# The samples' attention steps through its caches two sequences at a time instead of one

## Chip, cores, metric

One core of a Trainium2 chip runs the whole program. The metric is the device time of one execution in microseconds; the kernel before takes 2231.66 us (median of 3 runs, 2231.16 to 2231.71).

## What is computed

One layer of a decoder with a pair of half-step SwiGLU FFNs around a mixing block, for a prompt of 1024 tokens and for 8 sample sequences of 4 new tokens each. The part that matters here is the mixing block's softmax attention (8 heads of 64, three dilated windows). The prompt attends within itself; each sample sequence attends to its own cached keys and values, of which 896 positions fall in some window:

```python
s = jnp.einsum('bthd,btjhd->bthj', q, kg) * (Dh ** -0.5)
s = jnp.where(valid[None, :, None, :], s, -jnp.inf)
m = jnp.max(s, axis=-1, keepdims=True)
p = jnp.exp(s - m)
den = jnp.sum(p, axis=-1)
o = jnp.einsum('bthj,btjhd->bthd', p, vg) / den[..., None]
```

The second head group (gated linear attention), the FFNs and the output steps are untouched.

## The kernel before

Python generators, called streams, issue the instructions of the mixing block; each `yield t, wait` hands TensorE's place in the program to another stream. `Merge.run` (L767) is a planner that runs while the program is built: it keeps a clock, adds `t` to it and to the stream's `used`, holds the stream back until `wait` has passed, and then takes, of the streams that are ready, the one with the least `used / share`. So the order on each engine is fixed when the program is built, and the engines run it strictly in that order.

Four streams matter. `project` makes the projections (L883: twelve matmuls per turn). `attend` (L1421) is the prompt's attention, eight heads of seven tiles; a step issues score matmuls `st` (L1505, L1506), matmuls `sm` for the maxima of a later head (L1453, none in the last twelve steps), and, one or two steps late, the weighted sums `nd` (L1532) of tiles that VectorE has masked (L1516, L1518) and ScalarE has exponentiated (L1519). It loads the next heads' operands with DMAs on SP's queue (L1438 to L1444, L1395, L1397). `attend_sample` (L1603) works on two groups of four sequences. `scores` multiplies the group's queries with the cached keys: for each of four quarters and each of four sequences it takes a key tile `kc` of 128x4x224 numbers (448 KB) and issues four matmuls that each fill 32 of the array's 128 columns (L1641). `sums` does the same with value tiles `vc` (also 448 KB), seven matmuls each (L1689). `turn` and `turn_back` are transposes between them, `finish` the division at the end. All these tiles come from one ring of four buffers (`KV = 4`): SP issues a tile's DMA once the matmuls on the tile four places earlier are done. `mix_ahead` (L1766) starts the output projection on heads that are ready (L1791, `acc_wo`), from step 46 of attention on, and `mix_out` continues it: it loads the residual `h` (L1802), adds the results to it (L1820) and also multiplies the samples' rows (L1841, `acc_wos`).

Both `scores` and `sums` yield once per sequence, 64 times in all:

```python
                    yield 0.8, 0.5
```

One such turn is called a visit below: 32-column matmuls of the samples between full-width matmuls of another stream. A group's second scores begin before its first sums: `attend_sample` takes eight turns of `scores(1)` before it transposes group 0's weights.

Of the kernel before, what the change touches and what calls it, by code (L numbers as in the profile page):

```python
# [1602 lines left out]
def attend_sample(k, a):  # L1603


    nc = k.nc
    qs, ks = k.qs, k.ks
    att = k.new[:, 512:640].rearrange("p (a t) -> p a t", a=4)
    st = [Head(), Head()]

    def prepare(g):
        S = st[g]
        qz = S.qz = k.sa.tile([P, 5, 4, 32], F32, name=f"qz{g}", tag="qz", bufs=2)
        nc.gpsimd.memset(qz, 0.0)
        for hh in range(2):
            r = slice(64 * hh, 64 * hh + 64)
            src = qs[r, :, g * 16:g * 16 + 16].rearrange("p a (b t) -> p a b t", t=TS)
            nc.vector.tensor_copy(qz[r, 4].rearrange("p a (b h t) -> p a b h t", h=2, t=TS)[:, :, :, hh], src)
            for b in range(4):
                c0 = b * 8 + hh * TS  # L1620
                nc.vector.tensor_copy(qz[r, b, :, c0:c0 + TS], src[:, :, b])

    def fetch():
        g, hf, qu, b = order.pop(0)
        kt = k.sa.tile([P, 4, 224], F32, name=f"kc{g}{hf}{qu}{b}", tag="kv", bufs=KV)
        nc.sync.dma_start(kt, a["c_k"][g * 4 + b, 2 * hf + qu])
        keys.append(kt)

    def scores(g):
        S = st[g]  # L1630
        qz = S.qz
        m = S.m = k.sa.tile([P, 4], F32, name=f"sm{g}", tag="smx", bufs=2)
        for hf, (c0, c1) in enumerate(((0, 448), (448, NPOS + NS))):
            sc = k.sy.tile([P, 512], F32, name=f"ss{g}{hf}", tag="y")
            for qu in range(2):
                for b in range(4):
                    if not keys:
                        fetch()
                    kt = keys.pop(0)
                    for pr in range(4):  # L1640
                        nc.tensor.matmul(sc[32 * pr:32 * pr + 32, qu * 224:qu * 224 + 224], qz[:, b, pr], kt[:, pr],  # L1641
                                         start=b == 0, stop=b == 3, skip_group_check=True)
                    yield 0.8, 0.5
            if hf:
                for pr in range(4):
                    nc.tensor.matmul(sc[32 * pr:32 * pr + 32, 448:448 + NS], qz[:, 4, pr], ks[:, pr], start=True,
                                     stop=True, skip_group_check=True)
            else:
                S.s = k.sa.tile([P, NPOS + NS], F32, name=f"s{g}", tag="ssb")
            nc.vector.tensor_tensor_reduce(S.s[:, c0:c1], sc[:, :c1 - c0], k.mC[:, c0:c1], 1.0, -3e38, ALU.add,  # L1650
                                           ALU.max, accum_out=m[:, hf:hf + 1])
            if g == 0:
                if hf:
                    nc.vector.tensor_copy(k.mC[:, NPOS:NPOS + NS], k.mC[:, NPOS + NS:])
                else:
                    prepare(1)
            yield 0.3, 1.2
        nc.vector.tensor_tensor(m[:, 2:3], m[:, 0:1], m[:, 1:2], op=ALU.max)
        nc.vector.tensor_scalar(m[:, 2:3], m[:, 2:3], -1.0, None, op0=ALU.mult)
        nc.scalar.activation(S.s, S.s, AF.Exp, bias=m[:, 2:3], accum_out=m[:, 3:4])  # L1660
        yield 0.0, 0.5

    def turn(g, c):
        S = st[g]
        if c == 0:
            S.pT = k.pT
        ps = k.sm.tile([P, 512], F32, name=f"spt{g}{c}", tag="m")
        for i in range(4):
            w = min(P, NPOS + NS - (c + i) * P)
            nc.tensor.transpose(ps[:w, i * P:(i + 1) * P], S.s[:, (c + i) * P:(c + i) * P + w], k.ident)  # L1670
        if c == 0:
            nc.scalar.activation(k.pT[:, 0:4], ps.rearrange("p (c q) -> p c q", q=P), AF.Copy)
        else:
            nc.scalar.activation(k.pT[:, 4:7], ps[:, :3 * P].rearrange("p (c q) -> p c q", q=P), AF.Copy)
            nc.scalar.activation(k.pT[:NS, 7], ps[:NS, 3 * P:], AF.Copy)
        yield 0.9, 0.5

    def sums(g, pieces):
        S = st[g]
        if 0 in pieces:  # L1680
            S.pv = k.sy.tile([P, 512], F32, name=f"spv{g}", tag="y")
        for piece in pieces:
            for b in range(4):
                vt = k.sa.tile([P, 7, P], F32, name=f"vc{g}{b}{piece}", tag="kv", bufs=KV)
                nc.sync.dma_start(vt, a["c_v"][g * 4 + b, piece])
                for i in range(7):
                    c, pr = divmod(7 * piece + i, 4)
                    q = slice(32 * pr, 32 * pr + 32)
                    nc.tensor.matmul(S.pv[q, b * P:(b + 1) * P], k.pT[:, c, q], vt[:, i], start=b == 0 and c == 0,  # L1689
                                     stop=False, skip_group_check=True)  # L1690
                yield 0.8, 0.5
        if 3 not in pieces:
            return
        for pr in range(4):
            q = slice(32 * pr, 32 * pr + 32)
            nc.tensor.matmul(S.pv[q].rearrange("p (b d) -> p b d", d=P), k.pT[:NS, 7, q],
                             k.vs[:, None, pr * P:(pr + 1) * P].broadcast_to([NS, 4, P]), start=False, stop=True,
                             skip_group_check=True)
        yield 0.9, 0.5

    def finish(g):
        S = st[g]
        mE = k.sa.tile([P, 512], F32, name=f"mE{g}", tag="kv", bufs=KV)
        nc.sync.dma_start(mE, a["c_mE"])
        e = k.sa.tile([P, 640], F32, name=f"se{g}", tag="qz", bufs=2)[:, :512]
        nc.vector.tensor_tensor(e, S.pv, mE, op=ALU.mult)
        o = k.new[:, 640:704]
        nc.vector.tensor_reduce(o, e.rearrange("p (g d) -> p d g", d=64), mybir.AxisListType.X, ALU.add)
        nc.vector.reciprocal(S.m[:, 3:4], S.m[:, 3:4])
        nc.vector.tensor_scalar(o, o, S.m[:, 3:4], None, op0=ALU.mult)  # L1710
        yield 0.0, 1.0

    def turn_back(g, ps):
        nc.tensor.transpose(ps[:64, :P], k.new[:, 640:704], k.ident)
        for hh in range(2):
            nc.scalar.activation(
                att[64 - 64 * hh:128 - 64 * hh, :, g * 16:g * 16 + 16].rearrange("p a (b t) -> p a b t", t=TS),
                ps[:64, :P].rearrange("p (a b h t) -> p a b h t", a=4, h=2, t=TS)[:, :, :, hh], AF.Copy)

    def sample_end():  # L1720
        turn_back(1, k.acc.tile([P, 512], F32, name="sot1", tag="acc"))
        nc.vector.tensor_tensor(k.xs[:, 4:], *(x[:, 4:, SEQ:].bitcast(F32) for x in (k.xh, k.xl)), op=ALU.add)

    k.sample_end = sample_end
    def part_0():
        while k.held:
            yield None
        turn_back(0, k.sx.tile([P, 512], F32, name="sot0", tag="x"))
        yield 0.2, 0.5

    early, late = (0, 1, 2), (3,)
    order = [(g, hf, qu, b) for g in range(2) for hf in range(2) for qu in range(2) for b in range(4)]
    keys = []
    for _ in range(KV):
        fetch()
    prepare(0)
    yield 0.0, 9.0
    yield from scores(0)
    second = scores(1)
    for _ in range(8):  # L1740
        yield next(second)
    yield from turn(0, 0)
    yield from turn(0, 4)
    yield from second
    yield from sums(0, early)
    yield from turn(1, 0)
    yield from sums(0, late)
    yield from finish(0)
    yield from turn(1, 4)
    yield from sums(1, early)  # L1750
    yield from part_0()
    yield from sums(1, late)
    yield from finish(1)
# [519 lines left out]
def build(tc, a):  # L2273
# [155 lines left out]
    with tc.manual_schedule(engines=ENGINES):  # L2429
# [39 lines left out]
        nc.sync.dma_start(k.mC, a["c_mC"])  # L2469
        k.pT = k.sa.tile([P, PC + 1, P], F32, name="pT")  # L2470
        samples = Stream(attend_sample(k, a), 140)
        issue.run(proj, att, samples, until=lambda: proj.done)
        less_w(0)
# [180 lines left out]
```

## Time and profile before

| | |
|---|---|
| runs | 2231.16, 2231.66, 2231.71 us |
| profiled execution | 2235.7 us, span 2233.5 us |
| TensorE busy | 2164.3 us (97%) |
| VectorE, ScalarE, GpSimd busy | 1479.8, 814.2, 614.7 us |
| TensorE's granted clock, mean | 0.986 |
| samples' attention | first visit at 1099.8 us, last at 1291.7 us |

Times in the rows are microseconds from the span's start. A matmul in float32 leaves two records, so a visit of four matmuls has 8 and one of seven has 14; the duration of a record includes the time that it overlaps its neighbours, so the cost of a piece is read from start to start. The profile names what an idle engine waited for; TensorE's idle time is the one that counts as long as the chain that ends last runs over it.

### The profile page before, as it was taken

To read this page: it belongs to the slowest core of one execution; us is meant where nothing else is said; L and a number is where in the kernel's file an instruction comes from. 1 tells how busy PE (TensorE), PEld (TensorE's weight loads), DVE (VectorE), ACT (ScalarE), POOL (GpSimd) and SP (SyncE) were. 2 spreads that over 40 slices of the span, in tenths; PEclk is the share of its full clock that TensorE was granted. 3 is DMA by queue.
4 is the path that set the end of the run, shared out by engine and by line. 5 is a ranking of instruction groups with operands and counts; after the bars stand their busy time and mean duration, and the time that the engine had idled before them with its cause. 6 is when DMAs were issued, how large, how long until landed. Compare 5 with 4: busy or idle time off the path is not lost.

```text
span 2233.5 us, 40152 instructions
## 1 busy us (share of the span) xinstructions
PE 2164.3 (97%) x16446; PEld 1769.2 (79%) x16446; DVE 1479.8 (66%) x2472; ACT 814.2 (36%) x1377; POOL 614.7 (28%) x446
## 2 busy tenths in 40 slices
PE   7999999999999999989999999999999999999996
PEld 5788888877777899979877877778888887777875
DVE  7855655658888845675267545966565567888866
ACT  4433333333121634432145523433343333112554
POOL 0456656640000001100124400265665651000000
PEclk9999999999999999989999999999999999999998
DMA  3377676639683311134988742177667648775112
GB/s 118 114 260 247 230 255 237 221 136 411 229 296 114 115 41 35 66 115 158 285 229 245 216 168 105 50 243 260 243 223 260 239 146 329 307 264 198 67 48 78
DMA packets 139848, 424.48 MB, mean 190 GB/s; under 512 B 18480, under 2 KB 39600, under 8 KB 129040
## 3 DMA queue, kind: packets, MB, share of 16 engines
q1 hardware_dynamic: 130400, 340.49, 43.3%
q0 software_dynamic: 4096, 76.81, 10.2%
q10 hardware_dynamic: 5168, 4.61, 0.6%
q8 instruction: 129, 2.11, 0.4%
q14 instruction: 55, 0.45, 0.1%
HBM read 312.15 MB, written 176.75 MB: 219 GB/s over the span
## 4 chain that ended last, share of the span: by engine, by line
PE 60%; DVE 7%; ACT 4%; DMA 4%; issue 3%; POOL 0%; SPq 0%; DVEq 0%; ACTq 0%; POOLq 0%
PE acc_a_f L174 10%; PE acc_c_f L174 10%; PE acc_b_f L174 8%; PE acc_d_f L174 6%; PE acc_m L883 5%; PE acc_wo L1791 3%; PE acc_e_f L174 3%; PE nd L1532 2%; PE acc_b L94 2%; PE st L1505 1%; DMA QA<-d_q 1%; PE sm_f L315 1%; PE acc_k L873 1%; PE sd_f L552 1%; PE st L1506 1%
## 5 line engine op out<-in xcount | busy, mean ns | idle before, releaser
L281 POOL TENSOR_TENSOR S_f<-raw_gu_f,S_f 128x512 f32<-128x512 f32 x40 | 59.5, 1487 | 320.7 <-DVE wl_f_a L296 320.7
L296 DVE TENSOR_TENSOR wl_f_a<-raw_gu_f,wh_f_a 128x1024 fp32r<-128x1024 f32 x44 | 55.9, 1273 | 113.0 <-ACT wh_f_a L295 113.0
L354 ACT ACTIVATE g_f<-acc_a_f 128x512 f32<-128x512 f32 x44 | 26.3, 597 | 241.5 <-PE acc_a_f L174 240.2
L883 PE MATMUL acc_m<-wh_m,xh_mx 128*128 128x256 f32 x384 | 112.6, 293 | 0.0
L276 POOL TENSOR_TENSOR S_f<-raw_gu_f 128x512 f32<-128x512 f32 x40 | 54.1, 1351 | 204.0 <-DMA raw_gu_f<-w_gu 203.8
L883 PE MATMUL acc_m<-wl_m,xh_mx 128*128 128x256 f32 x384 | 109.5, 285 | 0.0
L883 PE MATMUL acc_m<-wh_m,xl_mx 128*128 128x256 f32 x384 | 109.0, 284 | 0.0
L174 PE MATMUL acc_b_f<-xd_f,wh_f_s 128*128 128x512 f32 x320 | 101.2, 397 | 3.9 <-DVE c_f L338 3.9
L174 PE MATMUL acc_b_f<-xd_f,wh_f_a 128*128 128x512 f32 x320 | 104.1, 406 | 0.0
L2061 POOL TENSOR_TENSOR ho_f<-ho_f,rbc 128x256 f32<-128x256 f32 x2 | 1.7, 886 | 363.9 <-DVE rbc L189 363.9
L174 PE MATMUL acc_b_f<-xc_f,wh_f_s 128*128 128x512 f32 x320 | 99.5, 392 | 2.2 <-DVE U_f L338 2.2
L560 ACT ACTIVATE wo_f_wh<-wr_f 128x1024 fp32r<-128x1024 f32 x34 | 36.0, 1058 | 144.3 <-DVE wr_f L338 56.7
L357 ACT ACTIVATE g_f<-g_f 128x512 f32<-128x512 f32 x44 | 27.9, 633 | 148.6 <-DVE g_f L338 148.6
L679 DVE SCALAR_TENSOR_TENSOR ho_f<-acc_d_f,ho_f 128x512 f32<-128x512 f32 x88 | 60.3, 688 | 32.2 <-PE acc_d_f L174 27.7
L560 ACT ACTIVATE wo_f_wl<-wr_f 128x1024 fp32r<-128x1024 f32 x34 | 36.0, 1059 | 124.5 <-DVE wr_f L338 34.1
L296 DVE TENSOR_TENSOR wl_f_s<-S_f,wh_f_s 128x1024 fp32r<-128x1024 f32 x40 | 76.9, 1924 | 5.3 <-ACT wh_f_s L295 5.3
L361 POOL TENSOR_TENSOR t_f<-c_f,t_f 128x512 f32<-128x512 f32 x44 | 76.3, 1733 | 7.9 <-issue 4.0
L883 PEld LDWEIGHTS acc_m<-wh_m,xh_mx 128*128 128x128 f32 x384 | 73.5, 191 | 3.8 <-issue 1.8
L174 PEld LDWEIGHTS acc_b_f<-xd_f,wh_f_s 128*128 128x128 f32 x320 | 60.6, 190 | 19.4 <-issue 5.6
L174 PE MATMUL acc_a_f<-xh_f,wh_f_a 128*128 128x512 f32 x176 | 70.2, 399 | 5.9 <-ACT xh_f L242 5.9
L360 POOL TENSOR_TENSOR c_f<-g_f,c_f 128x512 f32<-128x512 f32 x40 | 72.0, 1799 | 11.1 <-DVE c_f L338 11.0
L883 PEld LDWEIGHTS acc_m<-wh_m,xl_mx 128*128 128x128 f32 x384 | 73.9, 192 | 0.0
(620 smaller groups left out, 6738.4 us busy)
## 6 DMA issues: line engine op xcount, KB each, us to landing
raw_gu_f<-w_gu SPq DMA_DIRECT2D x42, 1024.0 KB, 5.4
xo_f_xh<-d_hid SPq DMA_DIRECT2D x36, 1024.0 KB, 10.2
xo_f_xl<-d_hid SPq DMA_DIRECT2D x34, 1024.0 KB, 8.1
o_kw<-k_win POOLq DMA_DIRECT2D x8, 4088.0 KB, 15.7
o_vw<-v_win POOLq DMA_DIRECT2D x8, 4088.0 KB, 15.8
d_hid<-c_f SPq DMA_DIRECT2D x88, 256.0 KB, 3.8
d_hid<-hi_f_t SPq DMA_DIRECT2D x88, 256.0 KB, 2.3
wr_f<-w_d SPq DMA_DIRECT2D x40, 512.0 KB, 6.2
```

What stands on the lines that cost most here:

```text
L94: k.nc.tensor.matmul(ps[:, :n], w[:, kt, col:col + P], x[:, kt, cs], start=kt == 0 and i == 0, stop=kt == nk - 1 and i == 2)
L174: k.nc.tensor.matmul(ps, w, x, start=first and n + i == 0, stop=last and n == len(kts) - 1 and i == 2, skip_group_check=True)
L276: pool(q.S[:, 0], q.A[:, 2], q.A[:, 3], op=ALU.add)
L281: pool(q.S[:, 1], q.A[:, 1], q.S[:, 1], op=ALU.subtract)
L296: dve(wl[:, b], src, wh[:, b].bitcast(F32), op=ALU.subtract)
L360: h1 = lambda u: pool(unit(u).c21, unit(u).g1, unit(u).c21, op=ALU.mult)
L361: sub = lambda x, y, z: pool(x, y, z, op=ALU.subtract)
L560: act(w[:, 0], A[p][PRODUCTS[i][2]], AF.Copy)
L679: nc.vector.scalar_tensor_tensor(o, b, 0.5, o, op0=ALU.mult, op1=ALU.add)
L883: nc.tensor.matmul(ps[:, :256], x[:, kt, at * P:at * P + P], wt[:, kt], start=kt == 0 and m == 0, stop=kt == KT - 1 and m == 2)
L1532: nc.tensor.matmul(out, V[:, VW * v:VW * v + P], H.pt[m][:, at:at + w], start=first, stop=(bk, n) in ((0, 3), (1, 6)), skip_group_check=True)
L1791: k.nc.tensor.matmul(ps, w[:, kt, m * P:m * P + P], x[:, kt, n * HT:n * HT + HT], start=kt == AHEAD_KT[0] and i == 0, stop=kt == 3 and i = ...
```

## The change

A sequence's turn no longer ends with a yield; every second one does, and counts double (1.6 instead of 0.8). The eight turns of `scores(1)` that are taken early become four, the same eight sequences' quarters. No instruction is added or removed; what changes is the order in which they stand on the engines and on SP's queue.

```diff
@@ scores
                     for pr in range(4):
                         nc.tensor.matmul(sc[32 * pr:32 * pr + 32, qu * 224:qu * 224 + 224], qz[:, b, pr], kt[:, pr],
                                          start=b == 0, stop=b == 3, skip_group_check=True)
-                    yield 0.8, 0.5
+                    if b % 2:
+                        yield 1.6, 0.5
@@ sums
                     nc.tensor.matmul(S.pv[q, b * P:(b + 1) * P], k.pT[:, c, q], vt[:, i], start=b == 0 and c == 0,
                                      stop=False, skip_group_check=True)
-                yield 0.8, 0.5
+                if b % 2:
+                    yield 1.6, 0.5
@@ attend_sample
     yield from scores(0)
     second = scores(1)
-    for _ in range(8):
+    for _ in range(4):
         yield next(second)
```

Lines behind the edits move by two (L1689 becomes L1690, L1791 becomes L1793).

**Sums beside attention, TensorE.** Of before (`vc` is a value tile, `pt` a tile of weights of the prompt's attention):

```order
L1689 MATMUL spv_11771<-vc_11772,pT 32x128 x7
L1505 MATMUL st_11781<-QA_10170,KA_10168 128x256
L1506 MATMUL st_11781<-QB_10175,KB_10173 128x256
L1505 MATMUL st_11781<-QA_10170,KA_10168 128x128
L1506 MATMUL st_11781<-QB_10175,KB_10173 128x128
L1453 MATMUL sm_11786<-KA_10915,QA_10916 128x512
L1453 MATMUL sm_11788<-KA_10915,QA_10916 128x512
L1532 MATMUL nd_11709<-pt_11748,gl 128x128 x4
L1689 MATMUL spv_11771<-vc_11810,pT 32x128 x7
L1505 MATMUL st_11819<-QA_10171,KA_10169 128x256
```

The same place now:

```order
L1368 MATMUL gt_11502<-ident,og 128x32
L1690 MATMUL spv_11506<-vc_11507,pT 32x128 x7
L1690 MATMUL spv_11506<-vc_11516,pT 32x128 x7
L1505 MATMUL st_11525<-QA_10964,KA_10963 128x256
L1506 MATMUL st_11525<-QB_10174,KB_10172 128x256
L1505 MATMUL st_11525<-QA_10964,KA_10963 128x256
L1506 MATMUL st_11525<-QB_10174,KB_10172 128x256
L1453 MATMUL sm_11530<-KA_10169,QA_10171 128x128
L1453 MATMUL sm_11530<-KA_10169,QA_10171 128x384
L1532 MATMUL nd_11533<-pt_11476,gl 128x128 x2
L1471 MATMUL pm_11545<-ident,mx_11188 8x128
L1690 MATMUL spv_11506<-vc_11555,pT 32x128 x7
```

One step of attention now separates two pairs of value tiles, where it separated two single ones; the samples go through their tiles twice as fast, counted in steps of attention. Over the whole stage the visits fall from 66 (32 of scores, 34 of sums) to 36 (18 and 18). The last value tile, which stood among the last matmuls of attention, now stands 19 of the 56 steps ahead of their end; 21 steps lie between the first and the last visit of the sums.

**The end of attention, TensorE.** Of before:

```order
L1689 MATMUL spv_12389<-vc_12673,pT 32x128 x7
L1532 MATMUL nd_12559<-pt_12634,gl 128x256 x2
L1532 MATMUL nd_12559<-pt_12670,gl 128x256
L1532 MATMUL nd_12559<-pt_12670,gl 128x128
L1791 MATMUL acc_wo_0_12498<-xh_mx,wo_11575 128x512
L1791 MATMUL acc_wo_0_12498<-xl_mx,wo_11575 128x512
L1791 MATMUL acc_wo_0_12498<-xh_mx,wo_11575 128x512
L1689 MATMUL spv_12389<-vc_12703,pT 32x128 x7
L1791 MATMUL acc_wo_0_12498<-xh_mx,wo_11575 128x512
```

The same place now:

```order
L1506 MATMUL st_12674<-QB_10175,KB_10173 128x128
L1532 MATMUL nd_12635<-pt_12658,gl 128x128 x4
L1532 MATMUL nd_12635<-pt_12670,gl 128x256 x2
L1532 MATMUL nd_12635<-pt_12691,gl 128x256
L1532 MATMUL nd_12635<-pt_12691,gl 128x128
L1793 MATMUL acc_wo_0_12713<-xh_mx,wo_11554 128x512
L1793 MATMUL acc_wo_0_12713<-xl_mx,wo_11554 128x512
L1793 MATMUL acc_wo_0_12713<-xh_mx,wo_11554 128x512 x2
```

Attention's last steps now stand alone, and all 96 matmuls of the output projection that were begun ahead (`acc_wo`) follow the last `nd`; before, 15 of them stood ahead of the last `nd` and 9 more between the last visits.

**The same place on SP's queue.** Of before (`raw_wo` are weights of the output projection, `mE` a mask that the samples' last step reads, `h` the residual in three pieces):

```order
L1685 DMA vc_12715<-c_v 128x896
L1704 DMA mE_12735<-c_mE 128x512
L1809 DMA raw_wo_12801<-w_out 128x2048
L1809 DMA raw_wo_12797<-w_out 128x2048
L1809 DMA raw_wo_12975<-w_out 128x2048
L1802 DMA h_12769<-d_h 128x8x352 x3
```

Now:

```order
L1443 DMA KB_10173<-d_k 64x1024
L1444 DMA QB_10175<-d_ql 64x1024
L1772 DMA gl<-w_out 128x2048
L1811 DMA raw_wo_12801<-w_out 128x2048
L1811 DMA raw_wo_12797<-w_out 128x2048
L1804 DMA h_12769<-d_h 128x8x352 x3
L1811 DMA raw_wo_12975<-w_out 128x2048
```

The residual's load stands ahead of the third weight tile, where it stood behind it, and the samples' own loads are all far ahead. At the projection's end the order of the key tiles is the same, and tile 4 still follows three loads of values (`gl`).

## Rows read from the trace of the kernel before

**Rows 1.** The page, parts 1 and 4: span, busy time of the engines, and the shares of the chain of work that ended last by engine.

```profile
span 2233.5 us, 40152 instructions
...
PE 2164.3 (97%) x16446; PEld 1769.2 (79%) x16446; DVE 1479.8 (66%) x2472; ACT 814.2 (36%) x1377; POOL 614.7 (28%) x446
...
PE 60%; DVE 7%; ACT 4%; DMA 4%; issue 3%; POOL 0%; SPq 0%; DVEq 0%; ACTq 0%; POOLq 0%
```

**Rows 2.** The timeline of TensorE in the projection stage around the fifth visit of the sample stream. Columns: start, duration (us), engine, line, operation, out<-in, form, count, and in brackets the idle time before it with what ended it.

```profile
1101.97 0.28 PE L883 MATMUL acc_m<-wh_m,xl_mx 128*128 128x256 f32 x1
1102.18 0.59 PE L1641 MATMUL ss<-kc,qz 128*32 128x224 f32 x8
1102.70 0.50 PE L1453 MATMUL sm<-KA,QA 128*128 128x512 f32 x1
1103.04 0.28 PE L883 MATMUL acc_m<-wh_m,xh_mx 128*128 128x256 f32 x1
1103.15 0.28 PE L883 MATMUL acc_m<-wl_m,xh_mx 128*128 128x256 f32 x1
...
1109.05 0.28 PE L883 MATMUL acc_m<-wh_m,xl_mx 128*128 128x256 f32 x1
1111.78 0.59 PE L1641 MATMUL ss<-kc,qz 128*32 128x224 f32 x8 [2.44 <-DMA kc<-c_k]
...
1113.03 0.42 PE L883 MATMUL acc_m<-wh_m,xl_mx 128*128 128x256 f32 x1
1113.25 0.42 PE L883 MATMUL acc_m<-wh_m,xh_mx 128*128 128x256 f32 x1
...
1114.66 0.98 PE L1641 MATMUL ss<-kc,qz 128*32 128x224 f32 x8
```

**Rows 3.** The same view at the end of the stage, in the output projection.

```profile
1318.33 2.26 PE L1841 MATMUL acc_wos<-gl,new 128*32 128x64 f32 x64 [3.04 <-ACT new L1716]
1320.52 0.80 PE L1791 MATMUL acc_wo<-xh_mx,wh_wo 128*128 128x512 f32 x1
...
1324.53 0.40 PE L1791 MATMUL acc_wo<-xh_mx,wh_wo 128*128 128x512 f32 x1
```

**Rows 4.** The same view beside attention: two transposes that mark the head boundary (L1471), and one visit of the weighted sums between attention's own matmuls.

```profile
1209.98 0.81 PE L1532 MATMUL nd<-pt,gl 128*128 128x256 f32 x4
1210.73 0.64 PE L1689 MATMUL spv<-vc,pT 128*32 128x128 f32 x14
1211.29 0.39 PE L1505 MATMUL st<-QA,KA 128*128 128x256 f32 x1
1211.52 0.28 PE L1506 MATMUL st<-QB,KB 72*128 72x256 f32 x1
1211.64 0.28 PE L1505 MATMUL st<-QA,KA 128*128 128x256 f32 x1
...
1212.62 0.27 PE L1471 MATMUL pm<-ident,mx 128*8 128x128 f32 x1
...
1232.10 0.27 PE L1471 MATMUL pm<-ident,mx 128*8 128x128 f32 x1
```

**Rows 5.** The same view in the projection stage, where two visits of 32 key matmuls stand back to back with a third (24 records; a visit of one sequence has 8).

```profile
1124.33 1.41 PE L1641 MATMUL ss<-kc,qz 128*32 128x224 f32 x24
```

**Rows 6.** The chain of work that ended last, in order of time (start, duration, what): the transfer that the fifth visit waited for.

```profile
1101.74 9.99 DMA kc<-c_k
```

**Rows 7.** The DMA view of 1187 to 1240 us (sums beside attention, head loads running). The q1 row is the queue of SP: packets, MB, share of 16 engines' time.

```profile
q1 hardware_dynamic: 5875, 13.35, 84.0%
...
vc<-c_v SPq DMA_DIRECT2D x16, 448.0 KB, 7.6
...
QB<-d_ql SPq DMA_DIRECT2D x3, 256.0 KB, 8.7
```

**Rows 8.** The DMA view of 1112 to 1130 us (projection stage). Columns of an issue: out<-in, queue, operation, count, KB each, median us from issue to landing.

```profile
kc<-c_k SPq DMA_DIRECT2D x8, 448.0 KB, 5.9
```

**Rows 9.** The DMA view of 1203 to 1222 us, the busiest stretch of that queue beside attention.

```profile
q1 hardware_dynamic: 2933, 5.25, 92.5%
```

**Rows 10.** The DMA view of 1256 to 1284 us (sums beside attention, no head loads left).

```profile
q1 hardware_dynamic: 1721, 5.49, 66.0%
...
vc<-c_v SPq DMA_DIRECT2D x12, 448.0 KB, 4.0
```

**Rows 11.** Busy time by engine in two stretches of one head each, the first with the pass for the maxima of a later head, the second without. Columns: PE, PEld, DVE, ACT, POOL busy us (instructions), granted clock, DMA share, GB/s.

```profile
1212.60:1232.10 19.50, 19.50 (x187) 16.24 (x185) 13.23 (x35) 10.32 (x20) 9.45 (x7) 1.00 0.93 278
1253.80:1275.30 21.50, 21.50 (x226) 16.82 (x223) 12.43 (x16) 13.98 (x25) 11.64 (x9) 1.00 0.68 215
```

**Rows 12.** The end of the stage, the chain in order of time: last weighted sum of attention, last step of the samples, and the load of the residual.

```profile
1287.19 0.93 PE nd L1532 x4
...
1297.28 0.18 DVE new L1710
...
1297.74 0.38 SPq L1802
...
1298.79 15.08 DMA h<-d_h
```

**Rows 13.** The timeline of VectorE there, columns as in the second group: the last write of attention's result.

```profile
1292.68 0.68 DVE L1563 TENSOR_TENSOR xl_mx<-fn,xh_mx 64x512 fp32r<-64x512 f32 x1 [0.70 <-ACT xh_mx L1562]
```

**Rows 14.** The timeline of TensorE in the output projection: a later one of the small matmuls of the samples.

```profile
1370.06 1.10 PE L1841 MATMUL acc_wos<-raw_wo,new 128*32 128x64 f32 x64
```

## The prediction

> **What bounds the kernel now.** The page comes first: TensorE is busy for 2164.3 of 2233.5 us, and of the chain that ended last 60% is TensorE's work [rows 1]. So a change counts as far as it shortens or lengthens TensorE's row of instructions, its waits included. It moves instructions only between the first visit (1099.8 us) and the samples' last matmuls in the output projection (1318.3 us); I read that stretch in TensorE's timeline, then the queue that feeds the ring, then the other engines, then the end. In the stretch TensorE hardly waits: 2.44 us for a key tile [rows 2] and 3.04 us at the end [rows 3] are its longest waits. That is the state which the change gives up: the ring of four tiles was asked for one tile per step, and will be asked for two.
>
> **Visits saved (a gain).** Between two projection matmuls lie 0.12 us from start to start; into a visit of keys it is 0.21, the visit takes 0.52 [rows 2]. Behind a visit the next matmul is slow by 0.11 (0.23 from start to start instead of 0.12 [rows 4]). So a lone visit costs 0.09 + 0.52 + 0.11 = 0.72 us. Standing behind another one it costs (1.41 - 0.59) / 2 = 0.41 [rows 5]. Each of the 14 visits of keys that go (32 to 18) saves 0.31: 4.3 us. A visit of the sums takes 0.56 [rows 4], with the same edges 0.76. Two of them back to back are not in the trace: no saving at all is one end, only the 0.26 that is left of 0.56 without a record's overlap of some 0.30 the other. In the ratio of the keys, 0.41 to 0.52, it is 0.44, which is the nearest row; 16 visits (34 to 18) save 0.32 each, 5.1 us. Together **-9.4 us**, between -4.3 and -12.
>
> **Waits in the projection stage (a loss).** Two tiles a turn bring the pair of tiles 4 and 5 to TensorE two turns after 1099.8. A turn took 2.36 us (1099.82 to 1102.18, the visits being 2.36 apart), one more tile makes it 2.77, so the pair is reached at 1105.4. Tile 4 was issued at 1101.74 and took 9.99 us [rows 6], behind the same loads as now; it lands at 1111.7. The wait is 6.4 us instead of 2.44: +4.0. Tile 5 is behind it in the same queue: it had landed when its own visit began at 1114.66 [rows 2], so it adds between 0 and 2.3 us; at the queue's 3.3 us per MB (13.35 MB in 84.0% of 53 us [rows 7]) a tile of 0.459 MB needs 1.5, of which the first half of the visit covers 0.6: +0.9. The six pairs behind it: a pair is requested when the pair two places earlier is done, and it is needed two blocks of twelve matmuls and a visit of 1.13 later, 2 x 1.43 + 1.13 = 4.0 us. A tile took 5.9 us to land here [rows 8], and the second of a pair lands up to 1.5 later. That is 1.9 to 3.4 per two pairs, three times, less what the longer block of 24 and the transposes give back; between 0 and 8, I take 2.5, near the shorter landing since the value loads are over by then. Sum **+7.4 us**, between 4 and 14.
>
> **Waits beside attention (a loss).** One head with its seven visits took 19.48 us (between the two transposes [rows 4]); without visits 19.48 - 7 x 0.76 = 14.2, or 2.0 per step. The sums now need 21 steps, 42.6 us, with 16 visits of 0.76 + 0.44 = 1.2 (19.2) and some 3 for their ends: 65 us of TensorE. The queue has in the same time 28 tiles (four come ahead), 12.9 MB, and three heads' loads of 1.6 MB and some 0.5 MB of values each, 6.3 MB: 19.2 MB at 3.3 us is 63 us, which is 97% of that time. The busiest stretch of 19 us so far had 92.5% [rows 9]; at that share it is 68.5, a loss of 3.5. By landing it is more: a pair is needed 2 x 2.0 + 1.2 = 5.2 us after its request. Where no head loads run, a tile landed in 4.0 us [rows 10], which is in time; beside them in 7.6, and the last of a head's loads took 8.7 [rows 7]. 2.4 us late, eight times (16 pairs, two to a turn of the ring), is 19; the five steps without a pair give back up to 10. So the ends are 0 and 19, and I take **+8 us**: the sums run beside head loads nearly throughout, so the 7.6 is nearer than the 4.0. The Trainium skill (DMA: Bandwidth & Descriptors, "Anatomy of one DMA") gives about 2.0 us plus bytes / 436e3 for one transfer, fitted on GpSimd's path: 3.05 us for a tile, 4.1 for two in a row. By it each pair would be in time and this term 0; the 7.6 us of the row speak against it here, and I keep the row.
>
> **Attention without company (a loss).** The last 19 steps stand alone, so TensorE has nothing between them to cover the other engines. A head with the maxima needs 14.2 us of TensorE and 13.2 of VectorE [rows 11]: nearly level, +0.5 for waits. A head without them took 21.5 us for ten visits of 0.76 and three pieces of the output projection (some 0.75 each), so 11.6 of TensorE alone, while ScalarE was busy for 14.0, of which 0.7 was the samples': 13.3, so +1.7. The last tile's mask, exponential and weighted sum have nothing beside them but eight matmuls: 0.5 to 1.8, I take 1.8 with the waits of the last five steps. Sum **+4 us**, between 0 (the engines work ahead) and 8 (twice that).
>
> **The end (a gain).** The residual's load was issued at 1297.74, once the samples' last vector instruction (1297.28) had let the weight tile ahead of it go; attention's last write had been done by 1293.4 [rows 12, 13]. Now it waits for attention alone, 5.5 us behind the last weighted sum (1287.19 + 0.68 to 1293.36) instead of 9.9, and lands 16.1 later [rows 12], 21.6 behind. TensorE has 120 matmuls of 512 columns there, 0.233 each, 28 us, before the small matmuls that waited 3.04 us [rows 3]; these need the chain of 4.5 us behind the load (1313.87 to 1318.33), so 26.1: in time by 2. The wait goes, and with it the lower level of TensorE's clock behind it: the small ones took 2.19 instead of 1.10 [rows 3, 14], and the next nine matmuls 4.01 us, 0.45 each (a 512-column matmul at 1.2 GHz) instead of 0.24, +1.8. Sum **-5.9 us**, and 0 if the load is later by 2 us or more.
>
> **Clock.** After 2.44 us of waiting the projection's matmuls fell to 0.22 from start to start for a while, half speed [rows 2]; that spell stays. New waits of that length bring new ones. One spell cost 1.8 to 2.9 (rows of the last paragraph), none is the other end: **+1.5 us**.
>
> **Sum.** -9.4 + 7.4 + 8 + 4 - 5.9 + 1.5 = +5.6 us. The profiled execution of 2235.7 us (span 2233.5) becomes 2241.3; it stands 4.0 us above the median of the runs, so the median of 2231.66 becomes **2237.3 us**, slower by 0.25%. About 0.2%, 4.5 us, is what a measurement of this kernel tells from no change.
>
> **Rivals.** (1) **The queue keeps up, and the kernel is faster.** If the second tile of a pair lands within 5.2 us beside attention and 4.0 in the projection stage, only the first wait is left: -9.4 + 4.0 + 1 - 5.9 = -10.3, 2221.4 us. For it speak the 4.0 us of the quiet stretch [rows 10], against it 84.0% of busy time while tiles were asked for half as often [rows 7]. The Trainium skill's formula above (DMA: Bandwidth & Descriptors, "Anatomy of one DMA") leads here. (2) **The end gains nothing**: the residual's load shares the queue with two weight tiles and lands 2 us later. Then +11.5, 2243.2 us. (3) **Attention alone is bound by ScalarE and VectorE**, and short waits pull the clock down twice: 8 instead of 4, and 5.8 instead of 1.5, gives +13.9, 2245.6 us. That the change does nothing is excluded by the order, 66 visits against 36.
>
> **Numbers.** Forecast 0.50, rival 1 0.26, rival 2 0.11, rival 3 0.10, others 0.03. The forecast's own spread is from -1 to +14, of which 0.21 lies within 0.2% and 0.29 above; rival 1 is faster but for 0.03 within; rivals 2 and 3 are slower but for 0.04 within; the others fall 0.01 to each side and within. So faster 0.24, the same 0.29, slower 0.47. The range reaches from 2222 (rival 1) to 2250 (forecast's end, with the tail gain lost).
>
> **What the profile would show.** Right: a wait of some 6 us for `kc` early, several of 1 to 2 us for `kc` and `vc`, VectorE and ScalarE as releasers in the last 19 steps, and no wait ahead of `acc_wos`. Wrong: no waits for `vc` beside the head loads (rival 1), a wait ahead of `acc_wos` of its old length (rival 2), or the stage from the first visit to the last weighted sum shorter than the 188 us it takes now.

## The result, and the profile after

The changed kernel takes 2261.63 us (median of four runs, 2259.62 to 2262.67) against 2231.68: a ratio of 1.0128, 95% interval 1.0116 to 1.0141. It is slower by 30 us where 5.6 were forecast, outside the range of 2222 to 2250. The profiled execution took 2259.6 us, 24 more than that of before (span 2257.8 against 2233.5); it stands 2.0 us below its median, that of before 4.0 above.

The page of the kernel after, against [rows 1]: TensorE works as long as before, and the rest of its time grew.

```profile
span 2257.8 us, 40152 instructions
...
PE 2165.4 (96%) x16446; PEld 1775.3 (79%) x16446; DVE 1482.3 (66%) x2472; ACT 813.8 (36%) x1377; POOL 614.1 (27%) x446
```

Five stretches of TensorE cut at the same instructions show where: first visit to attention's first `st`; to the `st` behind the last value tile; to the last `st`; to the end of the last `nd`; to the end of the last `acc_wo`. Columns: busy us (instructions), granted clock, DMA share, GB/s. The kernel before:

```profile
1099.82:1127.34 27.52, 23.89 (x217) 0.94 0.94 288
1127.34:1228.08 100.74, 98.63 (x792) 1.00 0.82 238
1228.08:1283.23 55.15, 55.15 (x518) 1.00 0.71 215
1283.23:1288.11 4.88, 4.18 (x38) 1.00 0.81 284
1288.11:1388.07 99.96, 96.83 (x666) 0.97 0.37 135
```

The kernel after:

```profile
1100.89:1137.70 36.81, 28.69 (x290) 0.91 0.96 323
1137.70:1264.38 126.68, 112.60 (x1045) 0.96 0.81 243
1264.38:1311.43 47.05, 40.74 (x229) 0.90 0.12 36
1311.43:1317.11 5.68, 3.39 (x24) 1.00 0.60 196
1317.11:1411.72 94.61, 94.61 (x644) 1.00 0.38 141
```

The stretches differ by +9.3, +25.9, -8.1, +0.8 and -5.4 us, together +22.6 of the 24. Two columns tell what it is. Idle time, which is length less busy, goes from 9.6 us to 30.8: +21.2. And the clock: the length times what the clock lacks of 1.00 is 1.7 + 3.0 = 4.7 us before (first and last stretch), 3.3 + 5.1 + 4.7 = 13.1 after (the clock has two digits, so the longest stretch is good to some 0.6 us). The waits of TensorE after (what was waited for, us in total, times, longest), where before had 2.44 for `kc` [rows 2] and 3.04 at the end [rows 3] as its longest:

```profile
PE spv L1690 <- DMA vc<-c_v: 11.6, 12, 2.8
PE ss L1641 <- DMA kc<-c_k: 7.2, 6, 5.1
PE nd L1532 <- ACT fn L1554: 2.6, 2, 2.2
PE nd L1532 <- ACT pt L1519: 2.3, 1, 2.3
PE sm L1453 <- DVE mx L1461: 1.8, 3, 0.8
PE sm L1453 <- ACT pT L1676: 1.5, 1, 1.5
PE st L1505 <- DVE pt L1516: 1.3, 1, 1.3
```

The timeline of TensorE after, the first and the fourth pair of the sums (the first waits in both of its halves, the fourth is undisturbed):

```profile
1186.75 0.64 PE L1690 MATMUL spv<-vc,pT 128*32 128x128 f32 x14 [1.50 <-DMA vc<-c_v]
1187.79 0.64 PE L1690 MATMUL spv<-vc,pT 128*32 128x128 f32 x14 [0.40 <-DMA vc<-c_v]
1188.36 0.56 PE L1505 MATMUL st<-QA,KA 128*128 128x256 f32 x1
...
1201.00 1.07 PE L1690 MATMUL spv<-vc,pT 128*32 128x128 f32 x28
1202.00 0.39 PE L1505 MATMUL st<-QA,KA 128*128 128x256 f32 x1
```

An undisturbed pair takes 1.00 us from start to start, with the edges of 0.20 [rows 2, 4] 1.20 instead of 2 x 0.76: 0.32 saved. With a wait inside, the second visit starts over: from 1187.79 it takes its full 0.57, and from start to start the pair comes to 1.20 instead of 1.00, the wait not counted; eight of the sixteen pairs had one.

The clock in eight stretches after (columns as above):

```profile
1111.50:1116.60 5.10, 4.76 (x28) 0.50 0.83 270
1164.50:1168.20 3.70, 3.67 (x18) 0.54 0.01 6
1188.30:1191.40 3.10, 3.10 (x25) 0.52 1.03 152
1225.40:1229.50 4.10, 4.10 (x16) 0.58 0.22 39
1263.40:1267.10 3.70, 3.69 (x23) 0.54 0.40 83
1304.00:1311.40 7.40, 7.34 (x30) 0.54 0.00 0
1242.00:1248.00 6.00, 4.02 (x54) 1.00 1.01 335
1316.10:1320.00 3.90, 3.81 (x18) 1.00 0.79 284
```

The first six are spells at half speed (0.50 to 0.58; 1.2 instead of 2.4 GHz); before there was one ahead of the end, from 1113.0 to 1116.2 at 0.50. Five of the six stand behind waits: 5.12 us for a key tile, 1.52 for `pT`, 1.50 and 0.40 and later 2.85 for value tiles, 1.25 and 2.18 in attention alone. The fourth began 6 us after the nearest wait, behind eight score matmuls of 128 columns. And from 1242 to 1248 TensorE stood still for 2 us in three waits, and at 1316.19 for 2.29 us at once, without any spell behind it. So most spells stand behind waits, and a wait does not tell whether one follows. The Trainium skill (TensorE: Matmul & The Clock Gate, "HAM oscillation — how this bites in real kernels") describes matmuls that start each tile at the lower clock, behind waits for a DMA of some 3 to 5 us. The row 1111.50, behind 5.12 us, agrees; the shorter waits of this case came out both ways.

The queue, 1180 to 1264 us after, against [rows 7, 9]:

```profile
q1 hardware_dynamic: 10286, 22.88, 91.8%
...
vc<-c_v SPq DMA_DIRECT2D x32, 448.0 KB, 6.5
```

For 84 us it was as busy as in its busiest 19 us before, and yet a tile landed in 6.5 us, no later than the 7.6 of before. What makes tiles late is also the order on SP. The timeline of SP near the last value tile, and TensorE there:

```profile
1255.17 0.33 SPq L1438 DMA_DIRECT2D KA<-d_k  x1
1255.55 1.09 SPq L1440 DMA_DIRECT2D QA<-d_q  x2
1256.68 0.58 SPq L1686 DMA_DIRECT2D vc<-c_v  x1
```

```profile
1259.93 0.64 PE L1690 MATMUL spv<-vc,pT 128*32 128x128 f32 x14
1263.41 1.04 PE L1690 MATMUL spv<-vc,pT 128*32 128x128 f32 x14 [2.85 <-DMA vc<-c_v]
```

The tile's place in the ring was free at 1252.9, but ahead of its load on SP stood a head's `KA` and `QA`, which waited for attention's `st` to release their buffers. The load was issued 3.8 us late, and TensorE waited 2.85. Over the sums SP stood still in front of such loads (what was waited for, us, times, longest):

```profile
SPq L1438 <- PE st L1506: 8.1, 4, 2.8
```

The end went as forecast: against [rows 3] no wait ahead of the small matmuls, which take 1.10 us, and full speed behind them (clock 1.00 in the last of the five stretches).

```profile
1344.96 1.10 PE L1843 MATMUL acc_wos<-gl,new 128*32 128x64 f32 x64
1345.99 0.50 PE L1793 MATMUL acc_wo<-xh_mx,wh_wo 128*128 128x512 f32 x1
```

### The profile page after: what moved, and what is told of

It is laid out like the page before. It is cut to its first block, busy times and chain, and to the rows that moved or that the text cites. A ratio compares the mean times of both kernels' runs of the same rounds, so it can differ in the third digit from the quotient of the medians.

```text
span 2257.8 us, 40152 instructions
## 1 busy us (share of the span) xinstructions
PE 2165.4 (96%) x16446; PEld 1775.3 (79%) x16446; DVE 1482.3 (66%) x2472; ACT 813.8 (36%) x1377; POOL 614.1 (27%) x446
## 4 chain that ended last, share of the span: by engine, by line
PE 41%; issue 13%; POOL 9%; DVE 6%; ACT 4%; DMA 4%; SPq 0%; DVEq 0%; ACTq 0%; POOLq 0%
PE acc_d_f L174 6%; PE acc_c_f L174 6%; PE acc_a_f L174 5%; PE acc_m L883 5%; PE acc_wo L1793 4%; PE acc_e_f L174 3%; POOL t_f L361 2%; DMA vc<-c_v 2%; PE acc_b L94 2%; POOL S_f L277 1%; POOL S_f L281 1%; POOL S_f L276 1%; POOL c_f L359 1%; PE nd L1532 1%; POOL c_f L360 1%
## 5 line engine op out<-in xcount | busy, mean ns | idle before, releaser
L1461 DVE CUSTOM_DVE_ANT_0 jk<-sm,mS 128x512 bf16<-128x512 f32 (+2 forms) x96 | 53.1, 553 | 34.1 <-PE sm L1453 31.6
```

What stands on the lines that cost most here:

```text
L1461: nc.vector.tensor_tensor_reduce(jk[:, :w], ps[:, at:at + w], k.mS[:, m0:m0 + w], 1.0, -3e38, ALU.add, ALU.max, accum_out=H.mx[:, pc * 8 + ...
```

## Experiments

Theory A, formed from the rows above: the pair of visits is a gain, and what costs is the pace. The edit lets the samples go through their tiles twice as fast per step of attention, so that tiles come late, and it leaves attention alone at the end. Rivals: B, the pair is the loss at any pace; C and D, attention alone is all of it, or none. The ratios are to the kernel before, run beside each on the same chip; its single runs there lay between 2224 and 2238 us, so medians of different tables are compared by their ratios.

**Pairs at the old pace.** In `scores` and `sums`:

```diff
-                        yield 1.6, 0.5
+                        yield 1.6, 1.8
```

> The change with the samples held back longer behind each pair (yield 1.6, 1.8 instead of 1.6, 0.5): one pair of tiles per two steps of attention, the pace in tiles of the kernel before, last pairs at step 54 of 56. Theory A (the loss is the doubled pace: tiles asked for faster than the queue brings them, half clock behind the waits, attention alone at the end): waits for tiles back to some 2.4 us, no wait of attention alone, visits save 30 x 0.33 = 10 us, so 2219 to 2226 us. Theory B (the pair is the loss: a ring of four holds two pairs only, so the second tile is late at any pace): waits for tiles stay above 8 us, 2235 to 2250 us.

Measured: 2224.77 us, ratio 0.9965 (0.9951 to 0.998), faster than before. The same edit again, beside the last three kernels:

> Pairs at the pace of before in both, once more beside the three others on the same chip: ratio 0.995 to 0.998, and if the two parts add, the sum of their gains to within 3 us.

Measured: 2226.99 us, ratio 0.9976 (0.996 to 0.9993). The waits of the first execution, for heads' loads, key tiles and value tiles:

```profile
PE sm L1453 <- DMA QA<-d_q: 4.7, 4, 2.5
PE ss L1641 <- DMA kc<-c_k: 2.8, 2, 1.9
...
PE spv L1690 <- DMA vc<-c_v: 0.6, 1, 0.6
```

Tiles wait for 3.4 us instead of 18.8, under theory B's 8, and the time falls below that of before, both times within the numbers given for it. B falls.

**Half the loads at the doubled pace.**

```diff
+                if b % 2 == 0:
+                    vt = k.sa.tile([P, 7, P], F32, name=f"vc{g}{b}{piece}", tag="kv", bufs=KV)
+                    nc.sync.dma_start(vt, a["c_v"][g * 4 + b, piece])
```

(In place of the two lines without a condition, and the same for `kc`. A ring of four tiles now reaches over four pairs.)

> The change with the second tile of each pair not loaded: both visits of a pair read the first one's tile (half the keys and values are left out), so half the loads, and the ring holds four pairs. Order of TensorE as in the change. Theory A: waits for tiles fall from 18.8 us to under 3, and the half clock behind them goes too (some 8 us); what is left above the kernel before is attention alone: 2230 to 2241 us. Theory C (the loss is attention alone in the last 19 steps, with ScalarE and VectorE as its bound; the tiles' waits only take time that would be waited for anyway): above 2250 us.

Measured: 2233.76 us, ratio 1.0003 (0.999 to 1.0016). 28 us of the loss hang on the tiles; C falls. No wait for a tile is left. The first three of the five stretches, cut as above (here the first runs from 1097.70):

```profile
1097.70:1124.45 26.75, 25.72 (x289) 1.00 0.92 300
1124.45:1234.28 109.83, 106.45 (x1045) 0.98 0.63 178
1234.28:1282.51 48.23, 42.56 (x229) 0.86 0.14 40
```

In the first two the idle time falls from 22.2 us to 4.4 and the clock's share from 8.4 to 2.2: with the waits for tiles, most of the half speed went too. The third is much as it was: 5.7 us idle (6.3 in the change) at a clock of 0.86 (0.90). The two waits of `nd` are 2.8 and 2.8 us in all (2.3 and 2.6 in the change).

**Both.** The two edits together.

> Both at once: pairs at the pace of before (1.6, 1.8, as in the first experiment) and the second tile of each pair not loaded (half the keys and values are left out, as in the second). Nothing is left of the tiles' waits and nothing of attention alone. Theory A (both cost, apart from each other): against the kernel before a ratio of 0.990 to 0.9955, 10 to 15 us under the kernel with half the loads and the doubled pace, which is then the price of attention alone, 11 us more or less instead of the 4 forecast. Rival D (attention alone costs little; with half the loads the rest came from the pairs themselves): within 4 us of that kernel.

Measured: 2220.23 us, ratio 0.995 (0.9933 to 0.9966). The four ratios make a table:

| | all tiles loaded | half of them |
|---|---|---|
| pairs at the doubled pace | 1.0128 | 1.0003 |
| pairs at the old pace | 0.9965 | 0.9950 |

From 1.0003 to 0.9950 is 12 us (the intervals allow 7 to 17): attention alone, where the tiles play no part. D falls. And loading all tiles costs 28 us at the doubled pace, at the old one some 3, which the intervals do not tell from nothing. In the five stretches of this kernel's profile 5.6 us are idle and the granted clock is 1.00 in each; half the loads at the doubled pace left 12.9 us idle, and some 10 us to the clock.

**One part at a time.** Pairs in the scores alone, then in the sums alone, each at the doubled pace (the other with its `yield 0.8, 0.5` after each sequence):

> One part of the change alone: pairs in the scores, single visits in the sums (they start at step 15 instead of 26 and end at step 51). Theory A: waits for key tiles as in the change (7 us) with their half clock, 14 visits of 0.34 saved, no waits for value tiles, four steps alone: 2228 to 2236 us. Theory C: no long stretch alone, so within 3 us of before as well, 2229 to 2234.

Measured: 2242.49 us, ratio 1.0035 (1.002 to 1.005), that is +8 us, over the +4 that was the upper end of both theories. Key tiles wait 6.8 us as expected, but value tiles wait too (2.4), single visits though they are: the faster scores bring the sums 11 steps forward. That this is the reason was not tested.

> The other part alone: single visits in the scores, pairs in the sums (steps 26 to 47). Theory A: value tiles wait 5 to 10 us beside the head loads with some 5 us of half clock, 16 visits of 0.33 saved, the end gains 6: 2229 to 2240 us. Theory C: eight steps alone instead of 19, so less than half of the loss of 30 us: under 2246 us, with no difference between the stretches with and without waits for tiles.

Measured: 2240.84 us, ratio 1.0031 (1.0018 to 1.0045), +7 us, by its ratio 2238.6, within A's numbers and C's. The parts do not add (+8 and +7, together +30); each at double pace moves the other's place too, and no run parts the two effects.

**The same parts at the old pace.** As above, with a wait of 1.5 behind a pair of sums, and of 1.8 behind a pair of scores:

> Single visits in the scores, pairs in the sums held back (1.6, 1.5), so that they spread over steps 26 to 55. Theory A: 16 visits of 0.33 us saved, value tiles in time, no long stretch alone: ratio 0.995 to 0.9985. Theory B (pairs cost by themselves): 1.000 to 1.003.

Measured: 2229.35 us, ratio 0.9989 (0.9977 to 1.0001).

> Pairs in the scores held back (1.6, 1.8), single visits in the sums. Theory A: 14 visits of 0.34 us saved and nothing at the end: ratio 0.9965 to 0.9995. Theory B: 1.000 to 1.003.

Measured: 2230.2 us, ratio 1.0001 (0.9986 to 1.0016). Both intervals reach into A's numbers and touch 1; the first lies between A's and B's, the second at the lower end of B's. Their gains add to 2 us, that of both at once is 5.4: over 3 apart, though within what the intervals allow. What a part gains by itself is not told apart from nothing here.

**Sums later.**

```diff
     yield from second
+    while k.steps_done < 30:
+        yield None
     yield from sums(0, early)
```

> The change with the sums held back until step 29 of attention: their pairs at the same doubled pace in steps 29 to 49, where fewer head loads run; 15 steps in the middle of attention alone, six at the end instead of 19. Theory G (attention alone costs at the end, where heads have no pass of maxima and ScalarE is busy for 13.3 of their 11.6 us of TensorE; in the middle TensorE covers it): two thirds of some 11 us of that loss go and half of the value tiles' 11.6 us: ratio 1.003 to 1.008. Theory H (attention alone costs the same anywhere): only the tiles' waits fall: ratio 1.008 to 1.012.

Measured: 2241.84 us, ratio 1.0046 (1.0029 to 1.0063): theory G. Waits for key tiles, value tiles, and of attention at the end:

```profile
PE ss L1641 <- DMA kc<-c_k: 8.8, 4, 6.2
PE spv L1690 <- DMA vc<-c_v: 6.0, 6, 1.9
PE nd L1532 <- ACT pt L1519: 1.7, 1, 1.7
```

The value tiles' waits fall from 11.6 to 6.0, those of `nd` for ScalarE from 4.9 to 1.7. Steps 14 to 28 stand alone now, with 2.2 us idle in 32 and the clock at 1.00:

```profile
1182.22:1214.27 32.05, 29.84 (x183) 1.00 0.62 171
```

So attention without company costs at its end, where heads have no maxima [rows 11], and hardly in the middle.

**Work put into the waits.** In the last 19 steps:

(The two matmuls stand there once in the change.)

```diff
+            for _ in range(2 if 7 * h + n > 36 else 1):
+                nc.tensor.matmul(ps[:, at:at + w], keys, queries, start=True, stop=False, skip_group_check=True)
+                nc.tensor.matmul(ps[:, at:at + w], keys2, queries2, start=False, stop=True, skip_group_check=True)
```

> The change with the score matmuls of the last 19 steps of attention issued twice each, to the same place with the same operands: some 17 us of work more for TensorE in the stretch where it stands alone (64 matmul pairs' worth at 6.5 us per head, 2.7 heads). Theory A (in that stretch TensorE loses some 11 us to waits for ScalarE and VectorE and to the half clock behind them, so work fits into it): slower than the change by 3 to 9 us only, ratio to before 1.014 to 1.018. Rival D (the stretch has little to give): by 14 to 20 us, ratio 1.019 to 1.023.

Measured: 2274.55 us, ratio 1.0187 (1.0161 to 1.0212): 13 us more than the change, between the two theories, and the intervals of both are too wide to choose. The stretch from the 38th `st` step to the last, of the change and of this kernel (columns as above):

```profile
1268.15:1311.43 43.28, 36.97 (x213) 0.92 0.12 37
```

```profile
1263.62:1319.00 55.38, 54.44 (x297) 0.87 0.10 29
```

The work did go into the waits: idle time falls from 6.3 us to 0.9. But the clock falls too, from 0.92 to 0.87, which is 7.2 us of the stretch instead of 3.5. Less waiting did not bring the clock back: TensorE was busy for 54.4 of 55.4 us, and still ran at half speed for a quarter of them. Of the four spells only the first stands close behind a wait of over a microsecond, 2.18 us for the last value tile. The others begin at 1274.7, 1294.9 and 1315.3, each within a microsecond of the end of sixteen back-to-back score matmuls of 128 columns, of which the change has eight; one of them:

```profile
1294.90:1298.10 3.20, 3.20 (x13) 0.51 0.00 0
```

So the added work brought spells of its own, and this run does not test the waits alone.

**Tiles asked for early.** Behind each visit's matmuls the next tile's load is written, keys and values in one list (the lines in the sums; the scores have the same call):

```diff
+                if order and (b, piece) != (3, 3):
+                    fetch()
                 if b % 2:
                     yield 1.6, 0.5
```

> The change with each tile asked for as soon as the ring has a place: its load stands in SP's order right behind the visit that frees the place, ahead of heads' loads that it followed before. TensorE's order is that of the change. Theory E (order of the queue: seven value tiles were issued 1.1 to 3.8 us late behind a head's loads that waited for their buffers, and 7.8 of the 11.6 us of waits are theirs): those waits go, with some of the half clock: ratio to before 1.005 to 1.010. Theory F (the queue is full: a tile takes 6 to 9 us beside the head loads whenever it is issued): waits for value tiles stay at 9 to 13 us, ratio 1.011 to 1.015.

Measured: 2257.86 us, ratio 1.0122 (1.0102 to 1.0142). Waits for a head's `QA`, key tiles, value tiles:

```profile
PE sm L1453 <- DMA QA<-d_q: 9.3, 2, 5.4
PE ss L1645 <- DMA kc<-c_k: 7.6, 5, 3.6
PE spv L1696 <- DMA vc<-c_v: 3.0, 3, 2.1
```

E was right on the mechanism (value tiles wait 3.0 us instead of 11.6) and F on the time: the head loads that now stand behind the tiles are late instead, 9.3 us. The three waits come to 19.9 us, where the change had 18.8 for its tiles: here the order only chose who waited. The same at the old pace:

> Pairs at the pace of before (1.6, 1.8) and each tile asked for as soon as the ring has a place, as in the kernel with early loads. Theory E (SP's queue is one line: what moves ahead pushes a head's loads back, and TensorE then waits for QA): tiles were nearly in time at this pace already, so no gain or a loss against pairs at that pace alone: ratio to before 0.997 to 1.001, QA waits over 4.7 us. Rival (the few late tiles, 3.4 us of waits, are all that is left to gain): ratio 0.993 to 0.996.

Measured: 2234.8 us, ratio 1.0018 (1.000 to 1.0036), by the ratios 9 us slower than pairs at that pace without it. That lies a little past E's upper end, and E's sign came, waits for `QA` over 4.7 us:

```profile
PE sm L1453 <- DMA QA<-d_q: 11.4, 5, 3.3
```

against, in the second run of pairs at the old pace,

```profile
PE sm L1453 <- DMA QA<-d_q: 1.9, 2, 1.1
```

That is 9.5 us more of waits for `QA`, of the 11.2 by which the spans of these two executions differ.

## Why the prediction was wrong, step by step

- **Visits saved, -9.4.** Right on the piece: 0.32 us per pair of sums and 0.35 of scores (such a pair takes 0.89, with 0.20 of edges, against 2 x 0.72), 10 us. What it left out: a pair of sums whose second tile is late loses 0.20 again; eight pairs, 1.6 us.
- **Waits for tiles, 7.4 + 8.** Right in sum, and that by luck: the key tiles cost 4.8 (7.2 less the 2.44 of before) instead of 7.4, the value tiles 11.6 instead of 8, together 16.4 against 15.4. Its reason was half of it. It had tiles landing 7.6 us after their issue; they landed in 6.5, but several were issued 1.1 to 3.8 us late behind a head's loads, which the step did not look for.
- **Attention without company, +4.** Mis-sized. The waits of the last 19 steps are 8.5 us against 0.7, and the clock lost 4.7 more there (0.90 in 47.05, of which some 1.3 stands behind the last tile's wait); the table of four gives 12 for both. The step compared an engine's busy time over a head (13.3 of ScalarE against 11.6 of TensorE). In the 13.3 stood 2.5 for weights of the output projection (`wo`), which are no part of attention, and in the change ScalarE was busy for 31.4 of the 49 us from 1268 to 1317. The waits came out of chains within a step: `nd` for ScalarE's read-out of the head before (`fn`) and for the exponential (`pt`), `st` and `pm` for VectorE.
- **The end, -5.9.** Right: wait and slow spell are gone, and the last stretch is 5.4 us shorter. Fifteen more matmuls (3.5 us) stand in it and three visits (2.7) no longer do, so 6.2 for the term.
- **Clock, +1.5.** This is the step that failed. It allowed for one spell more; there were five more, and the clock's share grew from 1.7 us (the end apart) to 13.1: +11.4. The forecast priced the waits at their length; against 21 us more of them, the profile has 11 us more lost to half speed. An estimate from the kernel before comes nearer: there 1.7 us were lost behind 2.44 of waiting [rows 2], and at that rate the 19.4 us of waits in the forecast cost some 13. It was not one execution's bad luck: the four of the change had mean clocks of 0.978 to 0.981, the 65 of the kernel before that were run beside the experiments 0.983 to 0.990. The signs that the prediction named for being right came (5.1 us for `kc`, waits for `vc`, ScalarE and VectorE as releasers, none ahead of `acc_wos`), and none of them was about the clock.
- **The sum.** -10 + 1.6 + 16.4 + 8 - 6 + 11.4 = +21.4, against the 22.6 of the five stretches. The other 6 us up to the medians' 30 are the two profiled executions' distances from their medians, and no row places them.
- **Rivals.** Rival 1 (the queue keeps up) is what happens at the old pace: 0.9965 and 0.9976 are 2224 to 2226 us, against its 2221.4. The Trainium skill's price of a transfer (DMA: Bandwidth & Descriptors, "Anatomy of one DMA", 3.05 us per tile by estimate) put every pair in time; the waits of 11.6 us for `vc` speak against it at this load. Rival 3 (attention alone, with spells) was the nearest, and its 8 us for the one were right; its 5.8 for the clock were half, so that it came to 2245.6, and the range ended where no case had priced the clock higher.

What stays open: that half speed costs 11 us is read from the granted clock. That most of it goes when the waits go is shown, by half the loads (8.4 to 2.2 us in the stretches of the tiles) and by both edits together (1.00 throughout). No run took the spells away and left the waits, and the one that filled the waits at the end brought new spells, so what calls a single spell is not settled. Nor did a run test the end's gain by itself; it is seen in the rows alone. Pairs at the old pace beat the kernel before by 0.24 to 0.35%, 5 to 8 us, short of the 16 that the saved visits and the end promise together. In the first of its profiles `QA` was waited for 4.7 us instead of 1.9, and the clock took 5.0 us ahead of the end instead of 1.7; where the rest goes no run shows.

## What to carry to other kernels

Handing over less often in an order that a planner builds changes the pace as well as the number of visits: look at how many tiles now pass per step, and hold the stream back to the old pace when only the visits are to be saved. Where waits are added to a busy TensorE, give the clock a term of its own with a wide upper end: here it was half as large as the waits. On a queue as busy as this one (91.8%), moving a load forward moved another one back.

## What the runs showed that was not expected

- Whether a wait of TensorE is followed by half speed varied within one execution: 1.50 + 0.40 us of waits led to a spell of 0.52, a wait of 2.29 us and three of 2 us together left the clock at 1.00, and one spell began 6 us after the last wait. Between kernels it varied too: with 31.1 us idle in the five stretches, tiles asked for early lost some 24 us to the clock in its profiled execution, the change 13.1 with 30.8.
- TensorE fell to half speed without waiting: three times just behind sixteen back-to-back score matmuls of 128 columns, with no wait in the 5 us before, in a stretch with 0.9 us of idle time in 55.
- A tile waited for inside a back-to-back pair of 32-column visits costs 0.20 us beside the wait.
- At a queue share of 91.8% the median tile landed sooner (6.5 us) than at 84.0% before (7.6 [rows 7]).
